# Half-weights prepared further ahead: sums formed early, four buffers for the halves, head work queued as single operations

## The chip, the core and the metric

The kernel runs on one core of one Trainium2 chip. In the profile, PE is TensorE (matmuls), PEld its weight loads, DVE is VectorE, ACT is ScalarE, POOL is GpSimd and SP is SyncE, which here only issues DMAs. The time of a run is the device time of the program in microseconds (us), and less is better. An engine takes its instructions in the order in which they were put into its queue; one that waits holds up all behind it.

## What is computed

One pre-RMSNorm layer whose token mixer is an mLSTM, all in float32, for 256 tokens of width 4096. Cut to what matters:

```python
h = rms_norm(x, norm_w)
u = h @ w_in                                  # 4096 x 16400: q, k, v, og, z and the gates
qk = silu(causal_dwconv(qk, conv_w, conv_b))  # four taps
# 8 heads: q, k of 256, v of 512; chunkwise decayed attention A = w_intra * (q k^T)
hc = (A v) / max(|A 1|, exp(-m))
y = rms(hc) * out_norm_w * sigmoid(og) * silu(z)
out = x + y @ w_out                           # 4096 x 4096
```

Nearly all of the arithmetic is in the two products with w_in and w_out.

## The kernel before, in words

**Precision.** A float32 operand is split into a high and a low half of a reduced format that PE reads quickly (`split`, L132: ACT copies to the high half, DVE subtracts to get the low half). A product is then three matmuls, high by high, high by low, low by high (`matmul3`, L137, lines L139 to L141).

**Stages.** The columns that the gates and head 0 need come first, by plain products (the loop from L514). All else is done by `project_pair` (L285): 19 pairs of column blocks, two blocks of 512 columns each. The order is: oz of head 0 (its og and z), then qkv and oz of heads 1 to 7 in turn, then four pairs of the output product (o0 to o3). A pair is 360 matmuls of 512 columns.

**Operands of a pair.** The 4096 rows are eight chunks. In four of them (`FAST`) the 2 by 2 block product over two token halves and two row halves is done with seven products instead of eight (P1 to P7), whose weight operands are blocks 11, 22, 21, 12 of the weights or sums of these; there are four sums of weights to a chunk, done in place on DVE (L246, L252, L255, L258). In the other four chunks four plain blocks are used directly, each by twice as many matmuls. So a pair has 28 fast operands with 6 matmuls each, 16 plain ones with 12 each, and 16 sums. Each block is 128 x 1024 float32, loaded by SP into one of seven raw buffers (tag `wraw`, L155); its halves stand in buffers of `whi` and `wlo`, three of each (L67, L146).

**The other side.** The scaled tokens of each chunk are split once into `lhs` (`build`, L190): for the products with w_in from x (`build_x`), for w_out from the heads' results, which are written to DRAM and read back (`build_y`, in the last pair with w_in).

**Head work.** After a pair `combine` (L313) adds up the seven PSUM banks, on ACT and DVE. What follows for a head (convolution `conv_qk`, decay, scores, values, normalisation) is a list of large stages, of which `project_pair` takes one after every eighth of a pair. The gating of a finished head (`gate_y`, L600) is written between two pairs.

**Order on the engines.** The text of the program gives each instruction a priority by its place; the framework lays out the order of each engine when the program is built, by taking, from what is ready in its own estimate of time and has a free buffer, the instruction that stands first. On the chip this order is fixed, and waits are on semaphores.

Of the kernel before, what the change touches and what calls it, by code (L numbers as in the profile page):

```python
# [19 lines left out]
P = 128  # L20
# [21 lines left out]
FAST = (0, 2, 4, 6)  # L42

ORDER = ("P1", "P3", "P2", "P5", "P7", "P6", "P4")
TAGS = ORDER

DSUM = 0
# [14 lines left out]
def mlstm_layer(ctx: ExitStack, tc: tile.TileContext, x, xT, norm_w, w_first, w_in, conv_w, conv_b, gate_b,  # L62
# [4 lines left out]
    wpool = ctx.enter_context(tc.tile_pool(name="wpool", bufs=3))  # L67
# [52 lines left out]
    def rsqrt(dst, src, n, tag):  # L120
# [6 lines left out]
        for it in range(4):  # L127
            nc.vector.tensor_mul(t, r, r)
            nc.vector.scalar_tensor_tensor(t, t, -0.5, src, op0=OP.mult, op1=OP.mult)
            nc.vector.scalar_tensor_tensor(dst if it == 3 else r, t, 1.5, r, op0=OP.add, op1=OP.mult)  # L130
# [23 lines left out]
    def load(name, w, off, n):  # L154
        raw = wpool.tile([P, RAW], F32, name=f"w_{name}", tag="wraw", bufs=7)[:, :n]  # L155
# [7 lines left out]
    stages = deque()  # L163
# [24 lines left out]
    lhs = {}  # L188

    def build(c, src):  # L190

        if c in FAST:
            flat = lhs_pool.tile([P, 2 * 7 * HK * P], F32R, name=f"lhs_{c}", tag=f"lhs{c}")
            L = flat.rearrange("p (two s j t) -> p two s j t", two=2, s=7, j=HK)
            a11, a12, a21, a22 = (src[:, j * HK:(j + 1) * HK, t * P:(t + 1) * P]
                                  for t, j in ((0, 0), (0, 1), (1, 0), (1, 1)))
            F = big(f"F_{c}", [P, 4, HK, P])
            nc.vector.tensor_sub(F[:, 0], a21, a22)
            nc.vector.tensor_sub(F[:, 3], a21, a11)
            nc.vector.tensor_sub(F[:, 1], a11, F[:, 0])  # L200
            nc.vector.tensor_sub(F[:, 2], a12, F[:, 1])
            t0 = src[:, :, :P].rearrange("p (s j) t -> p s j t", s=2)
            for s0, s1, v in ((0, 2, t0), (2, 3, a22.rearrange("p (s j) t -> p s j t", s=1)), (3, 7, F)):
                for a in range(s0, s1):
                    split(L[:, 0, a], L[:, 1, a], v[:, a - s0])
            names = ("P1", "P2", "P4", "P5", "P6", "P3", "P7")
            lhs[c] = {s: [[L[:, part, i, j, :] for part in range(2)] for j in range(HK)]
                      for i, s in enumerate(names)}
        else:
            flat = lhs_pool.tile([P, 2 * 3 * CK * P], F32R, name=f"lhs_{c}", tag=f"lhs{c}")  # L210
            L = flat.rearrange("p (two s j t) -> p two s j t", two=2, s=3, j=CK)
# [360 lines left out]
    def merged(*fs):  # L572
        def run():
            for f in fs:
                f()
# [94 lines left out]
```

## Time and profile before

| | us |
|---|---|
| median of three runs | 1843.99 (1841.7 to 1845.84) |
| the profiled execution, its own time | 1845.81 |
| its span, first to last instruction | 1844.1 |
| PE, DVE, ACT busy in the span | 1773.2, 1654.5, 1135.5 |

The span is 1.7 us shorter than the time of the same execution. A matmul in the profile is shown with its way through the array, so that matmuls that follow each other closely overlap; PE counts as busy as long as any is under way, and a short wait for an operand hides in that overlap. The length of a pair against its number of matmuls tells more than the busy share.

### The profile page before, as it was taken

To read this page: it belongs to the slowest core of one execution; us is meant where nothing else is said; L and a number is where in the kernel's file an instruction comes from. 1 tells how busy PE (TensorE), PEld (TensorE's weight loads), DVE (VectorE), ACT (ScalarE), POOL (GpSimd) and SP (SyncE) were. 2 spreads that over 40 slices of the span, in tenths; PEclk is the share of its full clock that TensorE was granted. 3 is DMA by queue.
4 is the path that set the end of the run, shared out by engine and by line. 5 is a ranking of instruction groups with operands and counts; after the bars stand their busy time and mean duration, and the time that the engine had idled before them with its cause. 6 is when DMAs were issued, how large, how long until landed. Compare 5 with 4: busy or idle time off the path is not lost.

```text
span 1844.1 us, 21723 instructions
## 1 busy us (share of the span) xinstructions
PE 1773.2 (96%) x7804; PEld 1410.7 (77%) x7804; DVE 1654.5 (90%) x1882; ACT 1135.5 (62%) x1303; POOL 12.1 (1%) x29
## 2 busy tenths in 40 slices
PE   9888999999999999999999999999998899999998
PEld 8766787777777878787878787878776668787776
DVE  5799999998999899989998989898989998989887
ACT  6565765665566556656666666566656665565654
POOL 0000000000000000000000000000000000000000
PEclk9899999999999999999999999999999999999999
DMA  9654465556555555565556555655556556766563
GB/s 365 230 189 171 161 220 188 196 174 216 193 183 180 197 192 184 189 200 188 184 198 209 185 187 197 205 183 183 194 194 214 177 189 217 236 210 233 189 206 126
DMA packets 107724, 365.67 MB, mean 198 GB/s; under 512 B 12128, under 2 KB 12512, under 8 KB 107616
## 3 DMA queue, kind: packets, MB, share of 16 engines
q1 hardware_dynamic: 105360, 356.95, 57.9%
q0 software_dynamic: 1968, 6.82, 1.0%
q8 instruction: 61, 1.00, 0.2%
q10 hardware_dynamic: 288, 0.52, 0.1%
q14 instruction: 47, 0.39, 0.1%
HBM read 356.38 MB, written 7.86 MB: 198 GB/s over the span
## 4 chain that ended last, share of the span: by engine, by line
PE 69%; DVE 19%; issue 7%; ACT 3%; DMA 2%; SPq 0%; DVEq 0%; ACTq 0%
PE P_qkv L140 9%; PE P_qkv L141 9%; PE P_qkv L139 9%; PE P_oz L140 9%; PE P_oz L141 8%; PE P_oz L139 8%; PE P_o L140 4%; PE P_o L141 4%; PE P_o L139 4%; DVE wl_oz_P L135 2%; DVE wl_oz L135 2%; DVE lhs L135 1%; DVE w_oz L246 1%; DVE wl_o_P L135 1%; DVE wl_o L135 1%
## 5 line engine op out<-in xcount | busy, mean ns | idle before, releaser
L134 ACT ACTIVATE wh_oz_P<-w_oz 128x1024 fp32r<-128x1024 f32 x224 | 237.6, 1061 | 109.0 <-PE P_oz L141 91.7
L135 DVE TENSOR_TENSOR wl_oz_P<-w_oz,wh_oz_P 128x1024 fp32r<-128x1024 f32 x224 | 270.8, 1220 | 20.2 <-ACT wh_oz_P L134 18.4
L135 DVE TENSOR_TENSOR wl_qkv_P<-w_qkv,wh_qkv_P 128x1024 fp32r<-128x1024 f32 x196 | 237.1, 1221 | 43.4 <-ACT wh_qkv_P L134 40.7
L134 ACT ACTIVATE wh_qkv_P<-w_qkv 128x1024 fp32r<-128x1024 f32 x196 | 208.1, 1062 | 82.5 <-PE P_qkv L141 73.2
L140 PE MATMUL P_oz<-wl_oz,lhs 128*128 128x512 f32 x512 | 205.1, 401 | 11.4 <-DVE wl_oz L135 10.3
L134 ACT ACTIVATE wh_oz<-w_oz 128x1024 fp32r<-128x1024 f32 x128 | 135.5, 1059 | 128.0 <-PE P_oz L141 74.0
L139 PE MATMUL P_oz<-wh_oz,lhs 128*128 128x512 f32 x512 | 190.7, 401 | 18.4 <-ACT wh_oz L134 17.4
L134 ACT ACTIVATE wh_qkv<-w_qkv 128x1024 fp32r<-128x1024 f32 x112 | 118.8, 1061 | 143.1 <-PE P_qkv L141 126.4
L141 PE MATMUL P_oz<-wh_oz,lhs 128*128 128x512 f32 x512 | 201.6, 394 | 0.0
L140 PE MATMUL P_qkv<-wl_qkv,lhs 128*128 128x512 f32 x448 | 178.7, 399 | 4.0 <-DVE wl_qkv L135 4.0
L140 PE MATMUL P_oz<-wl_oz_P,lhs 128*128 128x512 f32 x448 | 179.4, 401 | 1.1 <-DVE wl_oz_P L135 1.1
L139 PE MATMUL P_oz<-wh_oz_P,lhs 128*128 128x512 f32 x448 | 178.6, 403 | 2.0 <-ACT wh_oz_P L134 2.0
L141 PE MATMUL P_oz<-wh_oz_P,lhs 128*128 128x512 f32 x448 | 176.7, 394 | 0.0
L141 PE MATMUL P_qkv<-wh_qkv,lhs 128*128 128x512 f32 x448 | 175.7, 392 | 0.0
L135 DVE TENSOR_TENSOR wl_oz<-w_oz,wh_oz 128x1024 fp32r<-128x1024 f32 x128 | 156.1, 1219 | 21.1 <-ACT wh_oz L134 21.1
L139 PE MATMUL P_qkv<-wh_qkv,lhs 128*128 128x512 f32 x448 | 162.1, 395 | 4.8 <-ACT wh_qkv L134 4.8
L135 DVE TENSOR_TENSOR wl_o_P<-w_o,wh_o_P 128x1024 fp32r<-128x1024 f32 x112 | 135.3, 1222 | 24.6 <-ACT wh_o_P L134 23.1
L135 DVE TENSOR_TENSOR wl_qkv<-w_qkv,wh_qkv 128x1024 fp32r<-128x1024 f32 x112 | 136.6, 1220 | 21.8 <-ACT wh_qkv L134 21.7
L140 PE MATMUL P_qkv<-wl_qkv_P,lhs 128*128 128x512 f32 x392 | 155.2, 396 | 0.0
L134 ACT ACTIVATE wh_o_P<-w_o 128x1024 fp32r<-128x1024 f32 x112 | 118.9, 1061 | 58.9 <-PE P_o L141 56.1
L139 PE MATMUL P_qkv<-wh_qkv_P,lhs 128*128 128x512 f32 x392 | 152.8, 394 | 1.5 <-ACT wh_qkv_P L134 1.5
L141 PE MATMUL P_qkv<-wh_qkv_P,lhs 128*128 128x512 f32 x392 | 153.5, 391 | 0.0
(223 smaller groups left out, 3468.1 us busy)
## 6 DMA issues: line engine op xcount, KB each, us to landing
w_oz<-in_w_in SPq DMA_DIRECT2D x256, 512.0 KB, 4.3
w_qkv<-in_w_in SPq DMA_DIRECT2D x224, 512.0 KB, 4.3
w_o<-in_w_out SPq DMA_DIRECT2D x128, 512.0 KB, 4.4
wf<-in_w_first SPq DMA_DIRECT2D x15, 528.0 KB, 6.3
wf<-in_w_first SPq DMA_DIRECT2D x15, 512.0 KB, 6.6
xr<-in_x SPq DMA_DIRECT2D x8, 512.0 KB, 7.4
xn<-in_xT SPq DMA_DIRECT2D x8, 512.0 KB, 4.0
xo<-in_x SPq DMA_DIRECT2D x16, 256.0 KB, 5.1
```

The source lines that it names most:

```text
L134: nc.scalar.activation(hi, src, AF.Copy)
L135: nc.vector.tensor_sub(lo, src, hi.bitcast(F32))
L139: nc.tensor.matmul(ps, a[0], b[0], start=first, stop=False)
L140: nc.tensor.matmul(ps, a[0], b[1], start=False, stop=False)
L141: nc.tensor.matmul(ps, a[1], b[0], start=False, stop=last)
L246: nc.vector.tensor_add(raw["11"], raw["11"], raw["12"])
```

## The change

1. The buffers of weight halves (`whi`, `wlo`) become four of each, the raw buffers six.
2. The order of a fast chunk is written as `STEPS`: P1, then a plain block, P5 and P3, a plain block, P7, P6 and P2, a plain block, P4, a plain block. Each sum is written right after the operand that frees its target, at least one plain block ahead of the operand that is split from it. Before, the order was P1, P3, plain, P2, P5, plain, P7, P6, plain, P4, plain, and a sum was written just ahead of its use.
3. Head work, the seven reads of `combine`, the gating, the building of `lhs` and the stores of results become a queue of small entries. After each of the 44 operands of a pair, `pump` takes as many entries as empty the queue four operands before the end. A bank is used again only after its read has been taken (`unread`).
4. `build` makes three splits of 512, 256 and 1024 elements instead of seven of 256 for a fast chunk. The reciprocal square root takes three rounds of Newton's method instead of four.
5. In the first stage the sums of squares of x come one chunk earlier, and the first five `lhs` are built over four chunks instead of three. The rows of x that the result is added to are loaded after the pair instead of ahead of `combine`. The weights lie in DRAM in the order in which `STEPS` loads them.

```diff
-
-ORDER = ("P1", "P3", "P2", "P5", "P7", "P6", "P4")
-TAGS = ORDER
-
-DSUM = 0
+TAGS = ("P1", "P3", "P2", "P5", "P7", "P6", "P4")
+
+STEPS = (("load", "11"), ("use", "11", "P1"), ("load", "12"), ("add", "11", "12"), ("gap",),
+         ("load", "22"), ("add", "12", "22"), ("use", "11", "P5"), ("add", "11", "22"), ("use", "22", "P3"), ("gap",),
+         ("use", "12", "P7"), ("load", "21"), ("use", "11", "P6"), ("use", "21", "P2"), ("add", "21", "11"), ("gap",),
+         ("use", "21", "P4"), ("gap",))
...
-    wpool = ctx.enter_context(tc.tile_pool(name="wpool", bufs=3))
+    wpool = ctx.enter_context(tc.tile_pool(name="wpool", bufs=4))
...
-        for it in range(4):
+        for it in range(3):
...
-        raw = wpool.tile([P, RAW], F32, name=f"w_{name}", tag="wraw", bufs=7)[:, :n]
+        raw = wpool.tile([P, RAW], F32, name=f"w_{name}", tag="wraw", bufs=6)[:, :n]
...
+    queue = deque()
+
+    def pump(n=1):
+        for _ in range(n):
+            if queue:
+                queue.popleft()()
...
+            def sums():
+                nc.vector.tensor_sub(F[:, 0], a21, a22)
+                nc.vector.tensor_sub(F[:, 3], a21, a11)
+
+            def more():
+                nc.vector.tensor_sub(F[:, 1], a11, F[:, 0])
+                nc.vector.tensor_sub(F[:, 2], a12, F[:, 1])
+
+            def plain():
+                split(rows[:, 0, :CK], rows[:, 1, :CK], src[:, :, :P])
+                split(rows[:, 0, CK:CK + HK], rows[:, 1, CK:CK + HK], a22)
+
+            def split_sums():
+                split(rows[:, 0, CK + HK:], rows[:, 1, CK + HK:], F.rearrange("p s j t -> p (s j) t"))
+                names = ("P1", "P2", "P4", "P5", "P6", "P3", "P7")
+                lhs[c] = {s: [[L[:, part, i, j, :] for part in range(2)] for j in range(HK)]
+                          for i, s in enumerate(names)}
+                lhs_of[c] = of
+            return [sums, more, plain, split_sums]
...
+        def prepare(todo):
+            for step in todo:
+                if step[0] == "load":
+                    b = step[1]
+                    raw[b] = load(f"{name}_{c}_{b}", w, at + ("11", "12", "22", "21").index(b) * P * n, n)
                 else:
-                    nc.vector.tensor_add(raw["22"], raw["22"], raw["11"])
...
+        def run(before, b, s, after):
+            prepare(before)
+            h = operand(f"{name}_{c}_{s}", raw[b])
+            prepare(after)
             return [(s, [(lhs[c][s][j], b) for j, b in enumerate(by_k(h))])]
...
+    def project_pair(name, w, off, of, between=None):
+        ps = {}
         plain = [u for c in range(NCH) if c not in FAST for u in plain_steps(name, w, off, c)]
-        steps = sorted([((i + 0.5) / len(fast), u) for i, u in enumerate(fast)]
-                       + [((i + 1) / len(plain), u) for i, u in enumerate(plain)], key=lambda v: v[0])
-        total = len(fast) + 2 * len(plain)
+        steps = []
+        for c in FAST:
+            for group in fast_steps(name, w, off, c):
+                steps += group
+                if plain:
+                    steps.append(plain.pop(0))
+        assert not plain
...
+        for n, (c, make, cost) in enumerate(steps):
+            while lhs_of.get(c) != of:
+                pump()
             for s, prods in make():
+                if s not in ps:
+                    while s in unread:
+                        pump()
+                    ps[s] = bank(f"{s}_{name}", s)
                 for a, b in prods:
                     seen[s] += 1
...
+            if between is not None and left[c] == 0:
+                between(c)
+            pump(-(-len(queue) // max(1, len(steps) - 4 - n)))
...
-        tt(A[:, 0], ps["P2"], p1, op=OP.add)
-        tt(B[:, 0], B[:, 0], B[:, 1], op=OP.add)
-        tt(p1, ps["P6"], p1, op=OP.subtract)
-        tt(r7, r7, p1, op=OP.add)
-        tt(B[:, 0], B[:, 0], p1, op=OP.add)
-        tt(B[:, 1], B[:, 1], r7, op=OP.add)
-        tt(A[:, 1], ps["P4"], r7, op=OP.subtract)
-        return A, B
+        unread.update(("P2", "P6", "P4"))
...
+        return A, B, [read("P2", A[:, 0], ps["P2"], p1, OP.add), read("P6", p1, ps["P6"], p1, OP.subtract),
+                      read("", r7, r7, p1, OP.add), read("P4", A[:, 1], ps["P4"], r7, OP.subtract),
+                      read("", B[:, 0], B[:, 0], B[:, 1], OP.add), read("", B[:, 0], B[:, 0], p1, OP.add),
+                      read("", B[:, 1], B[:, 1], r7, OP.add)]
...
-        if 1 <= c < 5:
+        if c < 4:
             for t in range(NT):
-                row_squares(t, c - 1)
-        if c == 4:
+                row_squares(t, c)
+        if c == 3:
             load_params()
             row_stats()
-        if c >= 5:
-            for b in ((0,), (1, 2), (3, 4))[c - 5]:
-                build_x(b)
-    builds = deque((build_x, c) for c in range(5, NCH))
+        if c >= 4:
+            for b in ((0,), (1,), (2, 3), (4,))[c - 4]:
+                for part in build_x(b):
+                    part()
...
+    for c in range(5, NCH):
+        queue.extend(build_x(c))
+    queue.extend([gate_stages[0]] + conv_qk(0, u0) + gate_stages[1:] + hs)
...
+        A, B, todo = combine(f"{what}{h}", ps)
...
+            todo += [lambda t=t, B=B: split(V[0][:, t, :], V[1][:, t, :], B[:, t, :]) for t in range(NT)]
+            todo += conv_qk(h, A) + hs
...
+            def gate_1(A=A, B=B, sg=sg):
+
+                sg[0] = big("sg", [P, NT, NB])
                 nc.scalar.activation(A, A, AF.Sigmoid)
-                nc.scalar.activation(sg, B, AF.Sigmoid)
-                nc.vector.tensor_mul(B, B, sg)
-                nc.vector.tensor_mul(B, B, A)
-                finish(B)
-            gate_y()
-            stages.extend(turn(h))
+                nc.scalar.activation(sg[0], B, AF.Sigmoid)
+
+            todo += [gate_1, lambda B=B, sg=sg: nc.vector.tensor_mul(B, B, sg[0]),
+                     lambda A=A, B=B: nc.vector.tensor_mul(B, B, A)]
+            todo += finish(B) + turn(h)
+        queue.extendleft(reversed(todo))
...
+        def residual(i, n=n, xs=xs, cols=cols):
+            xs[i] = big(f"xo_{n}_{i}", [P, NT, NB])
             for t in range(NT):
-                nc.sync.dma_start(xo[:, t, :], x[t * P:(t + 1) * P, cols[i]])
-            xs.append(xo)
+                nc.sync.dma_start(xs[i][:, t, :], x[t * P:(t + 1) * P, cols[i]])
+
+        ps = project_pair(f"o{n}", w_out, n * D * 2 * NB, "y")
+        while queue:
```

The last lines of the diff's core queue the same work for the pairs with w_out: the loads of x, the seven reads of `combine`, four adds and stores, run during the next pair. `conv_qk` is cut into five entries for each half (transposes with the first tap, three taps twice, silu, split), `head` into seven entries, `finish` into two.

## Rows read from the trace of the kernel before

**Rows 1.** The page's busy times of the span.

```profile
PE 1773.2 (96%) x7804; PEld 1410.7 (77%) x7804; DVE 1654.5 (90%) x1882; ACT 1135.5 (62%) x1303; POOL 12.1 (1%) x29
```

**Rows 2.** Windows: length; PE, PEld, DVE, ACT, POOL busy; clock; DMA share; GB/s.

```profile
0.00:111.60 111.60, 100.86 (x594) 90.45 (x594) 79.36 (x144) 71.09 (x115) 1.70 (x10) 0.95 0.82 291
111.60:217.20 105.60, 96.18 (x401) 73.22 (x402) 98.88 (x134) 66.01 (x88) 0.00 (x0) 0.97 0.50 170
217.20:302.10 84.90, 83.79 (x365) 67.10 (x364) 76.17 (x85) 54.02 (x58) 0.69 (x1) 1.00 0.59 195
...
480.90:572.60 91.70, 90.12 (x399) 71.91 (x398) 85.54 (x107) 59.01 (x69) 0.00 (x0) 1.00 0.56 184
572.60:659.50 86.90, 85.36 (x369) 67.73 (x368) 77.42 (x72) 53.23 (x56) 0.53 (x1) 1.00 0.61 199
...
1374.10:1480.90 106.80, 94.88 (x398) 72.13 (x397) 104.34 (x152) 69.17 (x99) 0.00 (x0) 0.98 0.56 193
1480.90:1572.30 91.40, 86.87 (x370) 67.50 (x369) 82.32 (x87) 56.81 (x66) 0.00 (x0) 1.00 0.63 205
1572.30:1658.90 86.60, 84.82 (x361) 66.77 (x360) 76.53 (x72) 48.59 (x49) 2.18 (x4) 1.00 0.66 218
```

**Rows 3.** Windows: parts of an oz pair, of a qkv pair, of the first stage.

```profile
480.90:500.00 19.10, 17.94 (x78) 13.70 (x77) 18.95 (x21) 10.85 (x12) 0.00 (x0) 1.00 0.45 150
...
520.00:540.00 20.00, 20.00 (x93) 16.21 (x93) 19.81 (x25) 14.53 (x16) 0.00 (x0) 1.00 0.54 176
...
630.00:659.50 29.50, 29.50 (x129) 23.79 (x128) 23.66 (x22) 18.12 (x20) 0.00 (x0) 1.00 0.68 225
...
68.00:78.00 10.00, 6.64 (x21) 5.38 (x22) 6.26 (x18) 4.20 (x11) 0.00 (x0) 0.50 0.80 263
```

**Rows 4.** Who waited for whom, whole span: us in total, times, longest.

```profile
ACT wh_qkv L134 <- PE P_qkv L141: 126.4, 83, 2.4
...
PEld P_oz L139 <- ACT wh_oz L134: 29.0, 37, 3.5
...
PE pr L184 <- DVE diag L183: 3.9, 1, 3.9
...
PE P_oz L139 <- ACT r L451: 1.0, 1, 1.0
```

**Rows 5.** Timeline of DVE at a pair's start: start, duration, idle before.

```profile
482.83 1.22 DVE L246 TENSOR_TENSOR w_oz<-w_oz,w_oz 128x1024 f32<-128x1024 f32 x1
...
490.84 0.68 DVE L325 TENSOR_TENSOR r_qkv<-r_qkv,p_qkv 128x512 f32<-128x512 f32 x1
491.44 0.68 DVE L326 TENSOR_TENSOR B_qkv<-B_qkv,p_qkv 128x512 f32<-128x512 f32 x1
492.04 1.22 DVE L258 TENSOR_TENSOR w_oz<-w_oz,w_oz 128x1024 f32<-128x1024 f32 x1
493.18 1.22 DVE L135 TENSOR_TENSOR wl_oz<-w_oz,wh_oz 128x1024 fp32r<-128x1024 f32 x1
```

**Rows 6.** Timeline of ACT in the same stretch.

```profile
489.58 1.06 ACT L134 ACTIVATE wh_oz<-w_oz 128x1024 fp32r<-128x1024 f32 x1 [2.35 <-PE P_oz L141]
...
492.70 1.04 ACT L134 ACTIVATE wh_oz<-w_oz 128x1024 fp32r<-128x1024 f32 x1
```

**Rows 7.** Groups by form: count, busy, mean ns, idle before and releaser.

```profile
L246 DVE TENSOR_TENSOR w_o<-w_o,w_o 128x1024 f32<-128x1024 f32 x16 | 19.5, 1220 | 1.8 <-DMA w_o<-in_w_out 1.8
...
L402 DVE SCALAR_TENSOR_TENSOR acc<-pt,cw,acc 128x254 f32<-128x254 f32 x32 | 15.2, 476 | 0.2
...
L135 DVE TENSOR_TENSOR lhs<-F,lhs 128x256 fp32r<-128x256 f32 x32 | 12.5, 418 | 0.0
...
L135 DVE TENSOR_TENSOR lhs<-F,lhs 128x512 fp32r<-128x512 f32 x8 | 5.5, 682 | 0.0
...
L128 DVE TENSOR_TENSOR rs_t_h<-rs_r_h 128x2 f32<-128x2 f32 x32 | 5.1, 159 | 0.7
```

**Rows 8.** DMA issues: count, size, median us to landing.

```profile
w_o<-in_w_out SPq DMA_DIRECT2D x128, 512.0 KB, 4.4
```

More of the change, by code (lines that the diff above doesn't have):

```diff
@@ L203, in build @@
[L203 to L211, printed above, removed]
-            F = big(f"F_{c}", [P, CK, P])
+            F = big(f"F_{of}_{c}", [P, 4, HK, P])
@@ L229, in fast_steps, with lazy, run @@
+    def lazy(make, n):
+        made = []
+        def run(i):
+            if not made:
+                made.extend(make())
+            made[i]()
+        return [lambda i=i: run(i) for i in range(n)]
+    unread = set()
     def fast_steps(name, w, off, c):
@@ L270, in plain_steps @@
+        todo, group, groups = [], [], []
+        for step in STEPS:
+            if step[0] == "gap":
+                group[-1][-1].extend(todo)
+                groups.append([(c, lambda g=g: run(*g), 1) for g in group])
+                todo, group = [], []
+            elif step[0] == "use":
+                group.append((todo, step[1], step[2], []))
+                todo = []
+            else:
+                todo.append(step)
+        return groups
     def plain_steps(name, w, off, c):
@@ L386, in conv_qk, with one @@
     def conv_qk(h, u):
[L388 removed]
+        def one(i):
             ct0 = (0, QK // P)[i] + h * 2
[L390 to L406 removed]
@@ new lines, in taps, with run, silu @@
+            def taps(a):
+                def run():
+                    acc, pt, ct = t_["acc"], t_["pt"], ct0 + a
+                    for j in range(1, CONV):
+                        nc.vector.scalar_tensor_tensor(acc[:, a, j:], pt[:, a, :T - j], cw[:, 3 - j, ct:ct + 1],
+                                                       acc[:, a, j:], op0=OP.mult, op1=OP.add)
+                return run
+            def silu():
+                nc.scalar.activation(t_["sg"], t_["acc"], AF.Sigmoid)
+                nc.vector.tensor_mul(t_["acc"], t_["acc"], t_["sg"])
@@ L583, in mlstm_layer, with between @@
     for n, (what, h, _, _) in enumerate(pairs):
-        def between(c, share, n=n):
-            if builds and share * 8 > NCH - len(builds) - 5:
-                f, b = builds.popleft()
-                f(b)
-            if n == len(pairs) - 1 and c is not None and c < HEADS - 1:
-                build_y(c)
-        ps = project_pair(f"{what}{h}", w_in, off, between)
+        def between(c, n=n):
+            if n == len(pairs) - 1 and c < HEADS - 1:
+                queue.extend(build_y(c))
@@ L628, in blocks_of @@
+        queue.extend([lambda residual=residual: (residual(0), residual(1))] + res[2])
+        queue.extend([lambda i=i, t=t, store=store: store(i, t) for i in (0, 1) for t in range(NT)])
+    while queue:
+        pump()
 def blocks_of(w, s1, s2):
```

196 lines of the change are left out of this document (73 added, 123 removed).

## The prediction

> **What bounds the kernel now.** I read the page's busy times first, then windows cut at the starts of the pairs, then windows inside a pair, the waits, and the timelines of DVE and ACT at a pair's start.
>
> PE is busy 96% of the span and DVE 90% [rows 1]; neither says how much is lost. The pairs do. In a stretch where PE never stops it takes 129 matmuls in 29.50 us, 0.2287 us each [rows 3], so the 360 matmuls of a pair need 82.3 us. A pair of the output product takes 86.6 us [rows 2]: 4.3 us lost. A qkv pair has 369 PE instructions in the rows, 361 in an output pair; the 8 more are short transposes, for which I put half a matmul each, 0.9 us: need 83.2, taken 86.9, lost 3.7. An oz pair has 399, 38 more, 4.4 us by the same estimate: need 86.7, taken 91.7, lost 5.0. The first qkv pair takes 84.9 and loses 1.7 [rows 2].
>
> Where it is lost: at the pair's start. From 480.9 to 500.0 PE does 78 instructions in 19.1 us while DVE is busy 18.95; later in the pair PE is busy all the time, and from 630.0 to 659.5 DVE needs only 23.66 of 29.50 us [rows 3]. So DVE has time in the pair as a whole (85.5 of 91.7 us, 77.4 of 86.9, 76.5 of 86.6 [rows 2]) but not at the place where `combine` and the head work fall. It can't save up that time: ACT waits for PE to give back a buffer of `whi`, 126.4 us in one group alone [rows 4], so DVE is never more than the two further buffers ahead. The burst shows this: ACT begins a high half at 492.70, three head and sum operations stand in DVE's queue ahead of the low half, which begins at 493.18 [rows 5, 6].
>
> Three stages are limited by DVE's amount of work: the first oz pair (105.6 us, DVE 98.9), the last oz pair (106.8, DVE 104.3), and, behind it, the first output pair (91.4, DVE 82.3, PE's need 83.2) [rows 2].
>
> **The change, part by part.** On DVE an operation of 1024 elements starts 1.14 us before the next, one of 512 0.60 us (492.04 to 493.18, 490.84 to 491.44 [rows 5]); I count with these.
>
> *Four buffers.* DVE may finish three operands beyond the one on PE instead of two. Take an oz pair under the new order. Behind a qkv pair 26 entries wait, one taken after each operand, so they fall on the first 26 operands: two chunks of 15 large operations (7 fast halves, 4 plain, 4 sums) and 7 more, 37 x 1.14 = 42.2 us. The entries hold 13 operations of 512 (7.8 us), 12 taps of 0.476 (5.7 us [rows 7]), four on scores (about 1.9 us by size) and some 14 tiny ones of 0.159 (2.2 us [rows 7]): 17.6 us. DVE needs 59.8 us. PE needs 90 matmuls a chunk for two chunks and 30 more, 48.0 us, and 4.4 of head work: 52.4. DVE would be 7.4 us late if it began level. With three buffers it can begin four large operations ahead (plain block, P5, two sums), 4.6 us, which leaves 2.8; with four it adds P3 and a sum, 6.8 us, which leaves 0.6. In a qkv pair 14 entries hold 7 of 512, two of 1024 and two scalings, about 7.9 us, beside 20 large operations, 22.8: 30.7 against PE's 20.6 + 5.5 + 0.9 = 27.0; 3.7 late, within the lead. So by count nearly all of the loss in these pairs can go. The losses add up to 6 x 5.0 + 6 x 3.7 + 1.7 + 3 x 4.3 = 66.8 us. Bounds: nothing, since the lead must really be there at each pair's start, and all 66.8. I take 65%, 43.4 us, because the count leaves room but lumps stay (two sigmoids of 1024 in one entry on ACT, two gating products).
>
> *Sums ahead of use, new order.* The same four sums a chunk: no cost by amount. The order is less even: three sums stand in front of the second plain block, so DVE's need runs 2.5 us ahead of PE's steps at worst, against 1.1 in the old order (same counting). It eats lead, and is in the 65%.
>
> *Spread entries.* No instruction is added. The queue now ends by operand 26 or 14, where the stages before were spread over eighths of a pair; the count above has that.
>
> *Fewer instructions.* Three splits instead of seven: 7 x 418 = 2.93 us against 682 + 418 + 1220 = 2.32 [rows 7], 0.6 us for each of eight builds; one round of Newton is 3 x 0.159, 0.5 us for each of nine. Hidden in pairs where PE sets the pace; worth something in the three DVE-bound stages, some 2.5 us in the last oz pair and 1 in the first.
>
> *First oz pair.* 105.6 us against DVE's 98.9 less 1: 7.7 to have; without smooth feeding 0. I take 5. *Last oz pair and first output pair.* Building `lhs` of the results, gating and head 7 stay in the same two pairs. The last oz pair can fall to about 102, the output pair from 91.4 to about 84: 12 together at most; I take 7, since DVE enters the output pair with no lead.
>
> *Six raw blocks.* In the old order up to five were held at once (11, 22, 21, 12 and a plain one), leaving two for loads under way; in the new at most three, leaving three. A load lands after 4.4 us [rows 8], a block is used every 82.3 / 32 = 2.6 us: three under way cover 7.8 us. No cost; if the cover is gone each late block costs up to its lateness.
>
> *Moved steps.* Four loads of x now issue on SP after the first operand of the next pair, with the weight loads behind them; before they stood at the start of their own pair, where weight loads behind them were 1.8 us late in all [rows 7]. About the same, 0 to 2 us either way. The tail behind the last matmul keeps its adds and stores: 0, within 1 us.
>
> *First stage.* PE waits 3.9 us in it for the row statistics [rows 4], and from 68 to 78 us it runs at a granted clock of 0.50, with only 21 instructions [rows 3]; statistics come a chunk earlier here, and loads of x compete earlier. Between -9 (wait and slow stretch gone) and +6; I take -2. The Trainium skill (TensorE: Matmul & The Clock Gate, HAM oscillation) says that waits for data let TensorE's clock drop, so that what follows starts slow; the trace agrees, 0.50 right behind the wait. By that rule the first stage gains 5 us more as soon as the wait is short, and the total would be 1783.
>
> Sum: 43.4 + 5 + 7 + 2 = 57.4 us. From the profiled execution's 1845.8 that gives 1788. The median of the runs is 1844.0, 1.8 lower, so I don't claim the last two microseconds.
>
> **The rivals.** *Half of it (1808 to 1838).* The order is laid out from what is ready, so the old kernel already forms sums early (L246 at 482.83, ahead of the halves of its pair's first operands) and already mixes reads of banks with halves [rows 5]. Then only the fourth buffer is new: a third of 66.8 us, 22, 3 of the first oz pair and 4 behind it, 1817.
>
> *No change.* The lead is never filled, because ACT and DVE reach a pair's start late as before; gains and the less even order cancel: 1843 to 1846. Against it: DVE idles a fifth of the time from 630.0 to 659.5 [rows 3].
>
> *Slower.* PE's queue is in fixed order, and each head puts nine places into it (two sets of transposes, decay, scores, row sums, two values, two turns) that need a DVE or ACT result. Today PE loses next to nothing there (1.0 us in the one wait for `r` [rows 4]). If the result now comes one large DVE operation late at each, because single entries stand behind halves, it costs 72 x 1.14 = 82 us against 57: 1870. From 0.8 us a place on it eats the whole gain.
>
> **How the numbers follow.** Most of the loss gone (1764 to 1808): 0.58. Half: 0.22. No change: 0.06. Slower: 0.14. So faster by over 0.2% (what a measurement of this kernel can tell from no change) 0.80, same 0.06, slower 0.14. The likeliest, 1788, has its own range 1764 to 1808. All losses gone would be 1845.8 - 66.8 - 7.7 - 12 - 9 = 1750, which I don't believe; from 1764 to 1846 less than 2 in 10 is left out.
>
> **What would show it.** Right: oz pairs of 87 to 89 us, qkv pairs of 84 to 85, output pairs of 83 to 84; DVE waiting for ACT less before a pair's end; the waits of PE for `wh_oz` down to a third; the first oz pair near 100 us; a wait at the row statistics under 2 us. Wrong: pairs as long as before with DVE busy at their start (half or no change); PE waiting at transposes and scores (slower); DVE's sums waiting for loads (six buffers too few).

## The result and the profile after

| | before | after |
|---|---|---|
| median of 4 runs each | 1844.76 us | 1793.95 us |
| ratio, 95% interval | | 0.973 [0.9713, 0.9747] |
| span of the profiled execution | 1844.1 us | 1791.6 us |

The kernel is faster by 50.8 us; the forecast was 57.4 us, within its range. The busy times of the page, against [rows 1]:

```profile
PE 1756.1 (98%) x7804; PEld 1419.5 (79%) x7804; DVE 1655.5 (92%) x1823; ACT 1107.1 (62%) x1271; POOL 12.1 (1%) x29
```

The same PE instructions, 59 fewer on DVE and 32 fewer on ACT. Windows cut at the starts of the pairs, against [rows 2] (length; PE, PEld, DVE, ACT, POOL busy with their instructions; clock; DMA share; GB/s): the first stage, first oz, first qkv, a regular qkv, a regular oz, the last oz, the first output pair, a later one.

```profile
0.00:108.50 108.50, 99.10 (x595) 88.47 (x596) 82.74 (x141) 71.27 (x106) 1.69 (x10) 0.98 0.84 300
108.50:209.20 100.70, 94.81 (x409) 73.78 (x408) 96.96 (x123) 65.06 (x85) 0.00 (x0) 0.98 0.54 177
209.20:292.30 83.10, 82.17 (x359) 66.40 (x358) 75.46 (x79) 51.81 (x54) 0.69 (x1) 1.00 0.60 200
555.30:640.30 85.00, 84.83 (x370) 68.16 (x369) 78.32 (x72) 52.33 (x55) 0.53 (x1) 1.00 0.60 206
640.30:729.20 88.90, 88.90 (x398) 72.18 (x397) 85.06 (x104) 56.89 (x68) 0.00 (x0) 1.00 0.57 188
1335.80:1425.40 89.60, 88.47 (x393) 70.85 (x391) 86.68 (x108) 59.60 (x76) 0.00 (x0) 1.00 0.60 197
1425.40:1526.10 100.70, 93.91 (x369) 72.64 (x370) 97.34 (x111) 61.34 (x72) 0.00 (x0) 0.93 0.62 213
1526.10:1610.50 84.40, 83.78 (x362) 67.48 (x361) 77.20 (x72) 47.98 (x49) 2.17 (x4) 1.00 0.66 224
```

A regular oz pair went from 91.7 to 88.9 us, a qkv pair from 86.9 to 85.0, an output pair from 86.6 to 84.4. The last oz pair shrank by 17.2 us and the first output pair grew by 9.3: DVE's work slid from the one to the other, and together they gave 7.9. In the first output pair the granted clock is 0.93, against 1.00 before: PE runs there for some 14 us at the lower of its two levels (an estimate from 0.93). DVE is busy for 97.3 of its 100.7 us, so whether the clock cost anything there is not shown.

Parts of a pair and of the first stage, against [rows 3]: an oz pair's start, its end, and a slow stretch.

```profile
640.30:660.00 19.70, 19.70 (x89) 15.91 (x87) 19.63 (x25) 12.40 (x14) 0.00 (x0) 1.00 0.48 162
700.00:729.20 29.20, 29.20 (x130) 23.85 (x130) 26.16 (x36) 19.95 (x26) 0.00 (x0) 1.00 0.62 202
57.80:61.30 3.50, 3.50 (x14) 3.11 (x14) 3.50 (x10) 1.36 (x4) 0.00 (x0) 0.51 0.99 352
```

At the pair's start PE now does 89 instructions in 19.7 us where it did 78 in 19.1, with DVE as full as before. DVE came in with more ready: when PE has turned to the pair for good, about 2.5 us behind its start, two sums are done, where before the first was still under way (482.83 [rows 5]):

```profile
638.27 1.22 DVE L281 TENSOR_TENSOR w_oz<-w_oz,w_oz 128x1024 f32<-128x1024 f32 x1
640.88 1.22 DVE L281 TENSOR_TENSOR w_oz<-w_oz,w_oz 128x1024 f32<-128x1024 f32 x1
```

Late in the pair DVE works 26.2 of 29.2 us; before it was 23.7 of 29.5.

Who waited for whom, whole span, against [rows 4]:

```profile
ACT wh_oz_P L135 <- DVE w_oz L281: 85.7, 42, 4.5
ACT wh_qkv_P L135 <- PE P_qkv L142: 77.6, 92, 1.9
ACT wh_qkv L135 <- PE P_qkv L142: 66.0, 50, 2.1
ACT wh_o_P L135 <- DVE w_o L281: 32.1, 10, 4.6
PEld P_oz L140 <- ACT wh_oz_P L135: 8.8, 15, 2.5
PE first_P L140 <- ACT lhs L583: 7.3, 3, 3.4
PE P_oz L140 <- ACT wh_oz_P L135: 3.8, 4, 2.2
```

The wait for the row statistics is gone, but PE waits 7.3 us in the first stage for scaled tokens. And the largest wait of ACT is now one that was small: 85.7 us for a sum that DVE has not formed yet, against 14.4 us in all oz pairs before.

DVE's timeline at an oz pair's start, against [rows 5] (start, duration, engine, line, operation), and ACT's, against [rows 6]:

```profile
646.02 0.68 DVE L362 TENSOR_TENSOR p_qkv<-P_qkv,p_qkv 128x512 f32<-128x512 f32 x1
646.62 1.21 DVE L136 TENSOR_TENSOR wl_oz<-w_oz,wh_oz 128x1024 fp32r<-128x1024 f32 x1
647.75 0.68 DVE L362 TENSOR_TENSOR r_qkv<-r_qkv,p_qkv 128x512 f32<-128x512 f32 x1
648.35 0.68 DVE L362 TENSOR_TENSOR B_qkv<-B_qkv,p_qkv 128x512 f32<-128x512 f32 x1
648.96 1.22 DVE L136 TENSOR_TENSOR wl_oz_P<-w_oz,wh_oz_P 128x1024 fp32r<-128x1024 f32 x1
```

```profile
647.03 1.06 ACT L135 ACTIVATE wh_oz_P<-w_oz 128x1024 fp32r<-128x1024 f32 x1 [1.73 <-PE P_oz L142]
657.21 1.06 ACT L135 ACTIVATE wh_oz_P<-w_oz 128x1024 fp32r<-128x1024 f32 x1 [1.38 <-DVE w_oz L281]
```

Head work and halves alternate, as written. Groups by form, against [rows 7], and the loads, against [rows 8]:

```profile
L136 DVE TENSOR_TENSOR lhs_x<-F_x,lhs_x 128x1024 fp32r<-128x1024 f32 x4 | 4.8, 1212 | 0.0
L129 DVE TENSOR_TENSOR rs_t_h<-rs_r_h 128x2 f32<-128x2 f32 x24 | 3.7, 154 | 0.2
```

```profile
w_oz<-in_w_in SPq DMA_DIRECT2D x256, 512.0 KB, 4.3
```

**Marks.** In some of the kernels below matmuls of two neighbouring pairs are mixed on PE, so starts of pairs can't be compared. I use as mark of a pair the start of the last of the four copies by which ACT empties its banks. Two neighbouring marks in the changed kernel, output pairs, 84.4 us apart:

```profile
1605.90 0.58 ACT L357 ACTIVATE r_o<-P_o 128x512 f32<-128x512 f32 x1
...
1690.26 0.58 ACT L357 ACTIVATE r_o<-P_o 128x512 f32<-128x512 f32 x1
```

### The profile page after: what moved, and what is told of

Same layout as the page of the kernel before. It is cut to its first block, busy times and chain, and to the rows that moved or that the text cites. A ratio compares the mean times of both kernels' runs of the same rounds, so it can differ in the third digit from the quotient of the medians.

```text
span 1791.6 us, 21695 instructions
## 1 busy us (share of the span) xinstructions
PE 1756.1 (98%) x7804; PEld 1419.5 (79%) x7804; DVE 1655.5 (92%) x1823; ACT 1107.1 (62%) x1271; POOL 12.1 (1%) x29
## 4 chain that ended last, share of the span: by engine, by line
PE 86%; DVE 7%; ACT 3%; issue 2%; DMA 1%; SPq 0%; DVEq 0%; ACTq 0%
PE P_oz L140 11%; PE P_oz L141 11%; PE P_oz L142 11%; PE P_qkv L141 10%; PE P_qkv L142 10%; PE P_qkv L140 10%; PE P_o L141 5%; PE P_o L142 5%; PE P_o L140 5%; ACT wh_qkv_P L135 1%; PE first_P L140 1%; PE first_P L141 1%; PE first_P L142 1%; DVE wl_oz_P L136 1%; DVE wl_oz L136 1%
## 5 line engine op out<-in xcount | busy, mean ns | idle before, releaser
L135 ACT ACTIVATE wh_oz_P<-w_oz 128x1024 fp32r<-128x1024 f32 x224 | 233.8, 1056 | 166.2 <-DVE w_oz L281 85.7
L141 PE MATMUL P_oz<-wl_oz,lhs_x 128*128 128x512 f32 x512 | 202.7, 396 | 0.0
L142 PE MATMUL P_oz<-wh_oz,lhs_x 128*128 128x512 f32 x512 | 201.3, 393 | 0.0
L140 PE MATMUL P_oz<-wh_oz,lhs_x 128*128 128x512 f32 x512 | 195.2, 396 | 1.8 <-ACT wh_oz L135 0.9
L141 PE MATMUL P_oz<-wl_oz_P,lhs_x 128*128 128x512 f32 x448 | 179.0, 400 | 1.1 <-DVE wl_oz_P L136 1.1
L140 PE MATMUL P_oz<-wh_oz_P,lhs_x 128*128 128x512 f32 x448 | 175.9, 402 | 3.9 <-ACT wh_oz_P L135 3.8
L141 PE MATMUL P_qkv<-wl_qkv,lhs_x 128*128 128x512 f32 x448 | 177.4, 396 | 0.9 <-DVE wl_qkv L136 0.9
L142 PE MATMUL P_oz<-wh_oz_P,lhs_x 128*128 128x512 f32 x448 | 177.1, 395 | 0.0
L142 PE MATMUL P_qkv<-wh_qkv,lhs_x 128*128 128x512 f32 x448 | 176.1, 393 | 0.0
L140 PE MATMUL P_qkv<-wh_qkv,lhs_x 128*128 128x512 f32 x448 | 166.7, 393 | 0.0
L281 DVE TENSOR_TENSOR w_oz<-w_oz,w_oz 128x1024 f32<-128x1024 f32 x128 | 155.7, 1217 | 0.5
L141 PE MATMUL P_qkv<-wl_qkv_P,lhs_x 128*128 128x512 f32 x392 | 154.7, 395 | 0.0
L142 PE MATMUL P_qkv<-wh_qkv_P,lhs_x 128*128 128x512 f32 x392 | 154.2, 393 | 0.0
L140 PE MATMUL P_qkv<-wh_qkv_P,lhs_x 128*128 128x512 f32 x392 | 150.2, 398 | 1.1 <-ACT wh_qkv_P L135 1.0
```

What stands on the lines that cost most here:

```text
L135: nc.scalar.activation(hi, src, AF.Copy)
L140: nc.tensor.matmul(ps, a[0], b[0], start=first, stop=False)
L141: nc.tensor.matmul(ps, a[0], b[1], start=False, stop=False)
L142: nc.tensor.matmul(ps, a[1], b[0], start=False, stop=last)
L281: nc.vector.tensor_add(raw[step[1]], raw[step[1]], raw[step[2]])
```

## First round: which part is it

Theory A: the lead of the fourth buffer. Theory B: the spread entries. Theory C: the sums formed ahead.

**e1_buffers**, the kernel before with the buffers alone:

```diff
-    wpool = ctx.enter_context(tc.tile_pool(name="wpool", bufs=3))
+    wpool = ctx.enter_context(tc.tile_pool(name="wpool", bufs=4))
-  ... tag="wraw", bufs=7)
+  ... tag="wraw", bufs=6)
```

> The kernel before with one part of the change alone: four buffers of each weight half and six raw blocks. Theory A (the lead of DVE and ACT over PE was too short for the burst at a pair's start, and the fourth buffer lengthens it): 30 to 40 of the 51 us are here, 1805 to 1815 us, oz pairs near 89.5, qkv pairs near 85.5. Theory B (the lumps of head work were the loss, and cutting and spreading them is the gain): less than 10 us gained, 1835 us or more. Theory C (sums written ahead of use carry it): the same as B here.

1781.64 us, 0.965 [0.9635, 0.9664]: the buffers alone give more than the whole change, and far more than theory A put on them.

**e2_three**, the changed kernel with the old buffers (the same edit backwards):

> The changed kernel with three buffers of each half and seven raw blocks again, all else as changed. Theory A: 25 to 40 us are given back, 1820 to 1834 us, with waits of PE for halves at the pairs' starts. Theory B or C: under 10 us are given back, 1804 us or less.

1880.28 us, 1.0187 [1.0171, 1.0202]: everything but the buffers makes the kernel slower, by 34 us. That is above every range that was expected.

The same 172.9 us in the middle of each, two pairs of a head, in e1 and then in e2:

```profile
719.30:892.20 172.90, 172.90 (x767) 140.60 (x766) 161.19 (x178) 110.83 (x125) 0.53 (x1) 1.00 0.58 197
```

```profile
719.30:892.20 172.90, 166.99 (x720) 131.58 (x720) 155.27 (x165) 103.04 (x115) 0.53 (x1) 1.00 0.56 186
```

With four buffers and the old rest PE gets 767 instructions done and is never idle; with three and the new rest 720, and is idle for 5.9 us. Before it was 737, in the changed kernel 762.

**e3_order**, the changed kernel with the order of before and each sum right before its use:

```diff
-STEPS = (("load", "11"), ("use", "11", "P1"), ("load", "12"), ("add", "11", "12"), ("gap",),
...
+STEPS = (("load", "11"), ("use", "11", "P1"), ("load", "22"), ("use", "22", "P3"), ("gap",),
+         ("load", "21"), ("use", "21", "P2"), ("load", "12"), ("add", "11", "12"), ("use", "11", "P5"), ("gap",),
+         ("add", "12", "22"), ("use", "12", "P7"), ("add", "22", "11"), ("use", "22", "P6"), ("gap",),
+         ("add", "21", "22"), ("use", "21", "P4"), ("gap",))
```

> The changed kernel with the old order of operands and each sum right ahead of its use (STEPS rewritten), buffers and queue as changed. The prediction's count says the new order uses up lead (2.5 us at worst against 1.1): the old order is then the same or up to 5 us faster, 1789 to 1796 us. Theory C (a sum formed early takes a link out of the chain from sum to high half to low half to PE): slower by 10 us or more, 1804 us up. A third outcome, blocks landing late because the old order holds five of the six raw buffers: slower, with DVE or ACT waiting for loads.

1798.9 us, 0.9748 [0.9732, 0.9765]: 5 us slower than the changed kernel, 3 by the ratios, whose intervals overlap. It is outside the first two ranges. The third outcome is what its trace shows, DVE waiting 12.8 us for loads in two heads (the table below). That the old order holds five of six raw blocks can't be the whole reason: e9 has both and waits 1.0 us.

**e4_lumps**, the changed kernel with the head work in its old lumps at the old places:

```diff
-            pump(-(-len(queue) // max(1, len(steps) - 4 - n)))
+            done += cost
+            if done * NCH >= (popped + 1) * total:
+                popped += 1
+                pump()
...
-            todo += conv_qk(h, A) + hs
+            merged(*todo)()
+            queue.extend(lumps(conv_qk(h, A), hs))
```

> The changed kernel with the head work in the old lumps at the old places (reads of banks, splits of v, gating, stores of results at the pair's end, seven stages at eighths of a pair, building of the token side whole), buffers and sums as changed. Theory A: four buffers cover most of it, 1797 to 1808 us. Theory B: 1815 to 1835 us, with the loss at the starts of the pairs. In the last oz pair and the first output pair, whose work on DVE is the same, under 4 us change by either.

1798.44 us, 0.9742 [0.9727, 0.9757]. It is 4.5 us slower than the changed kernel, 2 by the ratios, with overlapping intervals. So A holds in its direction, with a larger effect than expected, and undoing B or C alone moves this kernel by 2 to 5 us, hardly clear of the noise. Neither brings back what e1 is ahead.

## Second round: what costs the 12 microseconds

One thing had been overlooked, in the forecast and so far here: `project_pair` of before spread the 16 plain uses evenly between the 28 fast ones by a sort; the changed one puts one plain use at each "gap". The order of before that the section on the change gives, with P7 and P6 next to each other, is that of e3; the sort puts a plain use between them. I write a chunk's uses with a bar for a plain one:

| | even mix | mix at the gaps |
|---|---|---|
| old order | P1 P3 \| P2 P5 \| P7 \| P6 P4 \| (before, e1) | P1 P3 \| P2 P5 \| P7 P6 \| P4 \| (e3) |
| new order | P1 P5 \| P3 P7 \| P6 \| P2 P4 \| | P1 \| P5 P3 \| P7 P6 P2 \| P4 \| (the change) |

**e5_new_order**, e1 with the new order and the early sums only:

```diff
-ORDER = ("P1", "P3", "P2", "P5", "P7", "P6", "P4")
+ORDER = ("P1", "P5", "P3", "P7", "P6", "P2", "P4")
...
+        before = {"P1": ("11",), "P5": ("22", ("12", "22"))}
+        after = {"P1": ("12", ("11", "12")), "P5": (("11", "22"),), "P7": ("21",), "P2": (("21", "11"),)}
```

> This is the kernel before with four buffers for the halves and six raw blocks, and of the rest only the new order of the seven uses and the sums formed ahead. With the buffers alone it took 1781.6 us, the whole change 1794.0. Theory O (the order and the early sums cost the 12 us, because ACT then stands before sums that DVE has not yet formed): about 1793, a mean steady pair of 87.0 us against 86.4, and the ACT wait for a DVE sum that the changed kernel shows comes up here too. Theory F (they are free or help, the cost is in how the program hands out the banks and mixes plain and fast uses): 1776 to 1783, a mean steady pair of 86.0 to 86.4.

1831.03 us, 0.9936 [0.9921, 0.9951]: it costs not 12 but some 50 of the 64 us, outside both ranges.

**e6_both_undone**, e4 with the STEPS of e3:

> The changed kernel with both the old order (sums right before their use) and the head work in lumps at its old places; what is left of the change are the four and six buffers, banks taken at their first use, the written mix of plain and fast uses, the wider splits and the earlier row loads. Each undone by itself gave 1798 to 1799. Theory O: with the order gone the cost is gone, about 1782. Theory F: the cost stays, 1797 to 1804, since what it blames is still in. If order and spread simply add up: 1803.

1796.5 us, 0.9744 [0.9725, 0.9762]. Theory O is out: the order is the old one and the cost is still there, as theory F had it.

**e7_merged**, e1 with the wide splits and three Newton rounds:

```diff
-            for s0, s1, v in ((0, 2, t0), (2, 3, a22.rearrange("p (s j) t -> p s j t", s=1)), (3, 7, F)):
-                for a in range(s0, s1):
-                    split(L[:, 0, a], L[:, 1, a], v[:, a - s0])
+            split(rows[:, 0, :CK], rows[:, 1, :CK], src[:, :, :P])
+            split(rows[:, 0, CK:CK + HK], rows[:, 1, CK:CK + HK], a22)
+            split(rows[:, 0, CK + HK:], rows[:, 1, CK + HK:], F.rearrange("p s j t -> p (s j) t"))
```

> The kernel before with four buffers for the halves and six raw blocks, and of the rest only the cheap part: the splits of the left factors in three wide pairs instead of seven narrow ones, and three Newton rounds for four. Both theories: the same steady pair of 86.4 us, and less DVE work where DVE is full, the first output-gate pair and the last one with the output factors. The wide splits save about eight short instructions for each fast chunk, and the rounds 0.9 us a head: 1777 to 1781 against 1781.6 for the buffers alone. Over 1783 and fewer, larger instructions hinder the neighbours more than they save.

1774.68 us, 0.9626 [0.9612, 0.9641], a little below the expected range: the fastest so far. Per head nothing changes; the first oz pair's mark comes 4.9 us earlier than in e1, and the last oz and first output pair take 187.0 for 190.0 us.

**e8_mix**, the changed kernel with the even mix:

```diff
-        for c in FAST:
-            for group in fast_steps(name, w, off, c):
-                steps += group
-                if plain:
-                    steps.append(plain.pop(0))
+        steps = sorted([((i + 0.5) / len(fast), u) for i, u in enumerate(fast)]
+                       + [((i + 1) / len(plain), u) for i, u in enumerate(plain)], key=lambda v: v[0])
```

> The changed kernel with plain and fast uses mixed evenly as before, and nothing else undone. Theory F, if the mix is the part that costs: 1782 to 1787 and a mean steady pair near 86.4 us (output pairs 83.6 against 84.4). Theory O: no change, 1792 to 1796, since DVE's sums still come late for ACT.

1838.98 us, 0.9974 [0.9963, 0.9985]: nearly all of the gain is lost. Both theories expected the wrong sign or none. The even mix is right for the old order and wrong for the new one, so order and mix have to be looked at together. The waits in two regular heads of e8, from 640 to 1000 us as in the table below, show what goes wrong:

```profile
ACT wh_qkv_P L135 <- DVE w_qkv L281: 28.0, 13, 2.6
ACT wh_oz_P L135 <- DVE w_oz L281: 19.6, 12, 2.7
```

In the new order the even mix puts three sums and the halves of P5 and P1 between two plain uses: P1's low half, 11+12, 12+22, P5's low half, 11+22. That is 5 x 1.14 = 5.7 us on DVE beside 12 matmuls, 2.7 us, on PE (durations from [rows 3, 5]); 3.0 us of lead are used up in one place, and ACT stands before a sum. With the gaps the worst place is 12+22, P5, 11+22, P3: 4.6 against 2.7, 1.8 us unrounded. The old order in the even mix has the same at worst (sum and half of P6, sum and half of P4).

The forecast counted in another way, and its count ranks the kernels better: DVE's operations from the start of a chunk up to a use, less PE's matmuls ahead of that use. At worst it gives 1.1 us for the old order in either mix, 2.5 for the new order at the gaps (7 operations, 24 matmuls) and 4.1 for the new order in the even mix (6 operations, 12 matmuls). These are estimates from the same durations. ACT's waits for sums in the table below have the same three levels: 1.6 to 11.0, 21.2 to 21.7 and 47.6 to 49.9 us.

## Third round: the mix, the spread, the row loads and the banks

Theory M: mix and order belong together. Theory S: the spread costs. Theory F2: the banks or the row loads cost.

**e9_spread_even**, e3 with the even mix (the edit of e8):

> The changed kernel with the old order of the seven uses and plain and fast uses mixed evenly as before (P7, a plain use, P6 and P4, where e3 has P7 and P6 together); the head work stays spread. Theory M (the mix and the order belong together; the old order wants the even mix): 1778 to 1785, a head near 172.8 us as with the buffers alone. Theory S (spreading the head work costs by itself): 1790 to 1799, a head of 173.5 or more, as e3.

1783.96 us, 0.9668 [0.9652, 0.9684]; a head takes 172.7 us. M, within its range.

**e10_lumps_even**, e6 with the even mix:

> The same with the head work in lumps at the old places, so that against e7 (1774.7 us) only the banks at first use, the order of the combining additions and the earlier row loads are left of the change. Theory M: 1775 to 1784, and what it takes less than e6 (1796.5 us) is the price of the mix. Theory F2 (the banks, the combining order or the row loads cost, not the mix): 1790 to 1798. Theory S: below e9 by 5 us or more.

1778.17 us, 0.9639 [0.9624, 0.9653]: against e6 the mix alone is 18 us; in e9 against e3 15. M for the mix. S also has its 5.8 us (e9 against e10), but at another place than it said: the heads are equal (172.7 and 172.9 us), and it is the last oz and the first output pair that take 192.8 us with the spread and 187.8 with lumps. PE's clock falls there with the spread, to 0.83 from 1415 to 1435 us in e9 against 1.00 in e10; how much of the 5 us that is was not tried.

What the gaps do to the old order is another wait. From 640 to 1000 us, first e6, then e10:

```profile
DVE w_oz L281 <- DMA w_oz<-in_w_in: 7.3, 6, 1.6
DVE w_qkv L281 <- DMA w_qkv<-in_w_in: 6.4, 6, 1.9
```

```profile
DVE w_oz L281 <- DMA w_oz<-in_w_in: 1.4, 2, 0.9
```

Here, in e6, DVE stands at a sum whose block has not landed, 13.7 us, and all low halves queue behind it.

**e11_rows**, e7 with the row loads, statistics and first builds a chunk earlier:

```diff
-        if 1 <= c < 5:
+        if c < 4:
             for t in range(NT):
-                row_squares(t, c - 1)
-        if c == 4:
+                row_squares(t, c)
+        if c == 3:
             load_params()
             row_stats()
-        if c >= 5:
-            for b in ((0,), (1, 2), (3, 4))[c - 5]:
+        if c >= 4:
+            for b in ((0,), (1,), (2, 3), (4,))[c - 4]:
                 build_x(b)
```

> e7 with the row loads, their statistics and the first builds one chunk earlier, as the change has them. The first stage and the first pair end at 191.8 us in e7 (by the last reading of that pair's banks), at 201.5 in e6. Theory M: the move takes part of those 10 us, since the row squares and the loads then fall where DVE and ACT already work at full for the first products: that mark at 195 to 200 us, the whole 1778 to 1783. Otherwise no change, 1773 to 1777, and the 10 us come from the banks or the mix.

1778.64 us (1777.95 to 1780.06), 0.9642 [0.9628, 0.9657], at the lower end of theory M's range. The intervals of e11 and e7 overlap; beside e12 on the same chip (1774.51 to 1775.88) it is 3.4 us slower, and its trace says where. The first mark comes at 199.7 instead of 191.8 us (the next pair gives back half). The wait of PE in the first stage, and the granted clock behind it, in e11 and then in e7:

```profile
PE first_P L139 <- ACT lhs L535: 8.2, 3, 4.1
```

```profile
99.20:102.60 3.40, 3.40 (x14) 3.01 (x13) 3.37 (x10) 1.26 (x4) 0.00 (x0) 0.51 0.88 343
```

```profile
PE first_P L139 <- ACT lhs L535: 2.9, 3, 1.5
```

```profile
99.20:102.60 3.40, 3.40 (x21) 2.81 (x20) 3.40 (x6) 2.81 (x6) 0.00 (x0) 1.00 0.12 48
```

The tokens of the next chunks come later: ACT waits longer for their loads, in e11 and then in e7, up to 110 us:

```profile
ACT lhs L535 <- DMA xT<-in_xT: 6.0, 4, 2.3
```

```profile
ACT lhs L535 <- DMA xT<-in_xT: 1.4, 2, 1.2
```

Which of the moved parts delays them was not tried one by one. Right behind a wait of 4.1 us PE runs for 3.4 us at the lower of its two clock levels (1.2 instead of 2.4 GHz).

**e12_banks**, e7 with banks taken at their first use and the bank-reading additions first:

```diff
-        ps = {s: bank(f"{s}_{name}", s) for s in TAGS}
+        ps = {}
...
+                if s not in ps:
+                    ps[s] = bank(f"{s}_{name}", s)
```

> e7 with the banks taken at their first use and the combining additions in the changed kernel's order (the three that read a bank first). Theory M: no loss, 1772 to 1777, since the three banks come free earlier and nothing else moves. Theory F2: 1785 or more, a head of 174 us or more, and the marks of the output pairs 84.4 us apart for 83.6.

1775.27 us, 0.9623 [0.9608, 0.9637]: no difference from e7. F2 is out for the banks, and right by 3 us for the row loads (with the statistics and first builds that moved with them).

All runs with four buffers, by time; each ratio is against runs of the kernel before in the same round. The last three columns are of stretches in the middle: PE instructions from 719.3 to 892.2 us, and from 640 to 1000 us ACT's high halves waiting for DVE's sums, and DVE's sums waiting for loads.

| kernel | order | mix | head work | us | ratio | PE instr. | ACT<-sum | sum<-load |
|---|---|---|---|---|---|---|---|---|
| e7 | old | even | lumps | 1774.7 | 0.9626 | 767 | 8.9 | 0.0 |
| e12 | old | even | lumps | 1775.3 | 0.9623 | 767 | 8.9 | 0.8 |
| e10 | old | even | lumps | 1778.2 | 0.9639 | 766 | 1.6 | 1.4 |
| e11 | old | even | lumps | 1778.6 | 0.9642 | 768 | 9.1 | 0.2 |
| e1 | old | even | lumps | 1781.6 | 0.965 | 767 | 9.6 | 0.7 |
| e9 | old | even | spread | 1784.0 | 0.9668 | 768 | 11.0 | 1.0 |
| the change | new | gaps | spread | 1794.0 | 0.973 | 762 | 21.7 | 0.0 |
| e6 | old | gaps | lumps | 1796.5 | 0.9744 | 762 | 4.4 | 13.7 |
| e4 | new | gaps | lumps | 1798.4 | 0.9742 | 763 | 21.2 | 0.0 |
| e3 | old | gaps | spread | 1798.9 | 0.9748 | 762 | 4.5 | 12.8 |
| e5 | new | even | lumps | 1831.0 | 0.9936 | 748 | 49.9 | 0.0 |
| e8 | new | even | spread | 1839.0 | 0.9974 | 743 | 47.6 | 0.0 |

Only the old order in the even mix reaches 766 to 768. Every other combination has more of one of the two waits at a sum. The waits rise with the loss; that they cause it is argued from the queues, since no run takes away a wait and leaves the rest as it is.

## Why the prediction came out right, and where its steps did not

**The sum.** By the marks the gain of the profiled executions, 52.5 us, divides like this (column e1: the buffers alone):

| | forecast | change | e1 |
|---|---|---|---|
| regular oz, qkv and output pairs | 43.4 | 36.0 | 43.2 |
| first stage and first oz pair | 7 | 10.5 | 12.6 |
| last oz and first output pair | 7 | 7.7 | 8.2 |
| tail | 0 | -1.7 | 0.0 |
| sum | 57.4 | 52.5 | 64.0 |

The tail did not grow: in every kernel here the last matmul ends 8.5 us before the end of the span. In the new order the marks come earlier within a pair, which adds to the line of the first stage and takes from the tail. By the starts of the pairs on PE the column of the change reads 36.6, 8.0, 7.9 and 0.

**Four buffers.** The mechanism is right, shown by e1 and e2. That 43.2 us in the regular pairs with the buffers alone meet the forecast's 43.4 is in part luck: its count gave nearly all of 66.8, and its 65% stood for lumps, which cost the regular pairs nothing (e9 and e10), and for a less even order, which e1 does not have. So the share held the cost of the order by chance: the regular pairs of the change gave some 7 us less than forecast, and the rest made up 2 of it. One reading was wrong as well. The low half that begins at 493.18 can't be that of the high half of 492.70, which lasts until 493.74; it belongs to the one of 489.58, done at 490.64, so it comes 2.5 us late and the burst is worse than was read. The pairs in e1 are nearly at PE's own need: 172.8 us a head against 83.2 + 86.7 = 169.9 by the forecast's count, 83.6 us an output pair against 82.3.

**Sums ahead of use, new order.** Here the forecast's step failed. It read the order as less even (2.5 us at worst against 1.1), put no price on that and left it in the 65%. With four buffers the order and its mix cost 10 us against the old order in its even mix (the change against e9). The regular pairs lost 7.2 us to the rest of the change (43.2 to 36.0), and ACT's 85.7 us of waiting for a sum in oz pairs is what a lead eaten at one place looks like; e9 has 44.7 of it, so it is the excess that goes with the loss. From 640 to 1000 us, the change and then e9:

```profile
ACT wh_oz_P L135 <- DVE w_oz L281: 20.2, 10, 4.0
```

```profile
ACT wh_oz_P L135 <- DVE w_oz L281: 10.4, 5, 2.7
```

A stretch of an output pair of the changed kernel shows how, DVE, the ACT instruction that waits, and PE's wait from 1620 to 1640 us:

```profile
1626.36 0.68 DVE L665 TENSOR_TENSOR xo<-xo,A_o 128x512 f32<-128x512 f32 x1
1626.96 1.21 DVE L136 TENSOR_TENSOR wl_o<-w_o,wh_o 128x1024 fp32r<-128x1024 f32 x1
1628.09 0.68 DVE L665 TENSOR_TENSOR xo<-xo,B_o 128x512 f32<-128x512 f32 x1
1628.69 1.21 DVE L281 TENSOR_TENSOR w_o<-w_o,w_o 128x1024 f32<-128x1024 f32 x1
```

```profile
1630.02 1.06 ACT L135 ACTIVATE wh_o_P<-w_o 128x1024 fp32r<-128x1024 f32 x1 [4.63 <-DVE w_o L281]
```

```profile
PE P_o L140 <- ACT wh_o L135: 0.5, 1, 0.5
```

The sum stands behind spread additions of the pair before; ACT is idle for 4.63 us before the high half that needs it, with the next ones queued behind; the lead is gone, and PE stops for 0.5 us. From 640 to 1000 us PE waits 0.4 us in the change and not at all in e9. The spread additions are not the cause as a whole: e4 has none and ACT waits as long for sums (21.2 us in two heads). By the count of the fullest stretch the changed order at the gaps and the old one in the even mix are equal (1.8 us each), so that count explains e5 and e8 alone. The forecast's own count, 2.5 against 1.1, goes with the last 10 us too (21.7 us of waits for sums against 11.0 in e9). So the forecast had the cost in its hands and took it to be within the lead. No run varies this count by itself.

**The mix of plain and fast uses** was in the diff and not in the forecast. By itself it is the largest term of all, with either sign: gaps instead of the even mix cost 15 to 18 us in the old order (e3, e6 against e9, e10) and save 45 in the new one (the change against e8).

**Spread entries.** "No cost" held for the regular pairs (e9 and e10: equal heads). In the last oz and the first output pair it cost 5 us in the old order and nothing in the new one (190.5 us in the change, 190.4 in e4). The 4.5 us by which the change is ahead of e4, 2 by the ratios with overlapping intervals, come in the first stage and first oz pair (mark at 198.8 us, 203.7 in e4).

**Fewer instructions.** 4.4 us by the ratios of e7 and e1 (0.965 less 0.9626, of 1844), 7 by their medians, forecast 3.5, and at the places named.

**First stage.** The wait for the statistics went, as forecast, but not by their coming earlier: in e1 they stand at the old place and the wait is gone, and in e2, with the earlier statistics and three buffers, most of its 3.9 us is still there:

```profile
PE pr L190 <- DVE diag L189: 3.3, 1, 3.3
```

Three waits for scaled tokens came in its place, 7.3 us against 2.8 before. The half-speed stretch is shorter than before but still there (0.51 from 57.8 to 61.3). e11 shows that the earlier row loads are a loss of 3 us, not a gain; that the stage gained came from the buffers (e1 has its first mark 2.1 us earlier than the change, though the marks of the change come earlier in a pair). The Trainium skill (TensorE: Matmul & The Clock Gate, HAM oscillation) has it that waits for data let the clock drop. The trace of e11 agrees, with 0.51 right behind its wait of 4.1 us, and e7, whose waits of that kind are 1.5 us at the longest, has 1.00 in the same stretch. The forecast of 1783 us by that rule had a short wait as its condition, which the change does not meet. The length of a wait alone does not settle it: in the changed kernel the clock fell behind a wait of 2.4 us (0.51 from 57.8), and behind one of 3.4 us it did not:

```profile
97.00:108.50 11.50, 11.50 (x73) 10.44 (x74) 10.90 (x22) 7.39 (x13) 0.00 (x0) 1.00 0.58 203
```

**Six raw blocks.** No cost in the forecast: the new order shows no sum waiting for a load, and e1 0.7 us in two heads. The old order at the gaps waits 13.7 us; why its loads come later there is not shown, and seven raw blocks with it were not tried.

**The rivals.** "Half" had its premise nearly right, that nothing but the fourth buffer helps, and its price wrong: it put 22 us on the buffer in the regular pairs and it was 43. "Slower" is what the change does with three buffers (e2), and not by the nine places of a head: PE has no wait of that kind in e2, where before it had the 1.0 us for `r`. The places are the sums, on which ACT waits 42.4 us in two heads of e2 and 4.5 before. Which of the order, the mix and the spread makes most of e2's 34 us was not tried.

**What the forecast said would show it.** Regular oz pairs at 89, qkv at 85, the first oz at 100.7, and PE's waits for the high halves of an oz pair (L139, L140) down to about a quarter: as named. DVE's waits for ACT's high halves, from 640 to 1000 us, fell from 29 to 17. The output pairs at 84.4 are above the 83 to 84.

**A better version.** e7, buffers with the wide splits and three rounds, is 69 us below before and some 19 below the change.

## What to carry to other kernels

When an engine that prepares operands has spare time over a stage but not at its start, one more buffer of lead can be worth more than any rearrangement: here 64 of 1844 us for two numbers. Before rearranging an order, count the preparing engine's operations against the work of the engine that it feeds: here the count from the start of a chunk up to each use, less what PE needs ahead of it, ranked the waits, where the fullest single stretch did not tell the change from the best order. An order and the mix it is dealt into can only be judged together, and an order that passes this count can still lose to late loads (e3, e6). Measure the buffer and the rearrangement apart, since a large gain from the one hides a loss from the other.

## What was not expected

- Moving one use of eleven across its neighbour (P6 before or behind a plain use) changed the time by 15 to 18 us: 11 to 13 us of DVE's waits for loads in two heads come and go with it.
- PE's instructions in 172.9 us of the middle rose from 737 to 767 with one more pair of half buffers, while DVE's busy time there rose only from 157.3 to 161.2 us: the time was there, only not in time.
